# Sums of weights moved into the pooling stage on GpSimd's DMA queue, with later operands, left sums and head norms re-placed

## Chip, cores and metric

The kernel runs on one core of a Trainium2 chip. The metric is the time on the device in microseconds (us) of one launch: three executions were timed, and one more was taken with the hardware profiler. Smaller is better. A core has TensorE (PE, matrix products), VectorE (DVE), ScalarE (ACT), GpSimd (POOL) and SyncE (SP), which here only issues transfers. Each engine executes its own instructions in the order of its own queue.

## What is computed

One layer of a hybrid decoder on 4096 tokens of width 1024, float32:

```python
def rmsnorm(x, w):
    y = xf * lax.rsqrt(jnp.mean(xf * xf, axis=-1, keepdims=True) + EPS)
    return (y * w)

def pool_mixer(u, pool_w, pool_scale):
    cs = jnp.cumsum(uf, axis=1)
    for g, win in enumerate((2, 4, 8, 16)):
        seg = cs[..., 256 * g:256 * (g + 1)]
        prev = jnp.pad(seg, ((0, 0), (win, 0), (0, 0)))[:, :S]
        outs.append((seg - prev) / jnp.minimum(pos, win) - uf[..., 256 * g:256 * (g + 1)])
    return jnp.einsum('bsgc,gcd->bsgd', jnp.stack(outs, axis=2), pool_w) * pool_scale

def mlstm_branch(mx, mz, mo, ...):
    xc = jax.nn.silu(causal_conv(mx, conv_w, conv_b))
    q, k, v = headwise(xc, w_q), headwise(xc, w_k), headwise(mx, w_v)
    h = mlstm_chunkwise(q, k, v, i_pre, f_pre)          # 4 heads, chunks of 128 tokens
    h = jax.nn.sigmoid(mo) * h
    hn = (h - mean(h)) * lax.rsqrt(var(h) + EPS) * mh_norm_w      # per head of 256
    return (hn + m_skip * xc) * jax.nn.silu(mz)

def reference(x, ...):                                  # x: 1 x 4096 x 1024, float32
    u = rmsnorm(x, norm_w)
    proj = u @ w_in                                     # 1024 x 5120
    pool_x, pool_z, m_x, m_z, m_o = the five 1024-wide parts of proj
    y_pool = pool_mixer(pool_x, pool_w, pool_scale) * jax.nn.silu(pool_z)
    y_mlstm = mlstm_branch(m_x, m_z, m_o, ...)
    x = x + jnp.concatenate([y_pool, y_mlstm], axis=-1) @ w_out   # 2048 x 1024
    return rmsnorm(x, final_norm_w)
```

## The kernel before

**Precision.** Every float32 operand of the large products is split into two parts that PE takes at its fast rate: hi is the value cast on ACT, lo is the value less hi, a subtraction on DVE (`split`, L107 to L111; ACT's cast is L110, DVE's subtraction L111). A product is then three matmuls, hi x hi, hi x lo and lo x hi (`mm3`, L113 to L119).

**Pooling stage** (L383 to L575). Eight blocks `b` of 512 tokens. Of each block the tokens are normalised (`norm_u`, begun in the block before) and split (`make_u`). Then eight columns `j` of 128 channels follow: 24 matmuls for pool_x (with pool_w and the scale folded into the weights), 24 for pool_z. ACT copies pool_x into the tile `z` (two buffers), GpSimd copies the last 16 tokens of the column before in front of it and saves its own last 16 (`halo`, L535 and L536), DVE makes the window sums and the product with the gate, and SP stores the result into `yp_d` (L560). PE's two results of a column lie in PSUM banks (`acc`, six buffers). The normalised tokens are stored in `us_d`.

**The four passes** (`drive`, L212) are the large products of the last stage: `o1` (y_pool times the first half of w_out, plus x, into `r_d`), `mo` (u times the m_o columns; gates the mLSTM's result, norms its heads, transposes them on PE with `turned`), `mz` (u times the m_z columns; gives y_mlstm into `ym_d`) and `o2` (y_mlstm times the other half of w_out, plus `r_d`, then the last norm). Each uses a Strassen scheme: seven half-size products in place of eight. Its left operand is four quadrants a11, a12, a21, a22 and four sums of them, s1 to s4 (`A_OF`), its right operand three quadrants of the weights and four sums of quadrants. A pass runs over four rounds `r` of 1024 tokens; a round has 14 steps (seven products `i`, two halves `kh`), each of 24 matmuls. `items` take the results of a product away and add them up (`after`, `done`).

**Where the sums come from.** The left sums of `us_d` and `yp_d` are made in the pooling stage by `sums` (L488 to L509): four loads of 512 KB on SP (L493) into the tiles `st` (four buffers), four operations on GpSimd, four stores (L497). The main loop starts such a job at the columns in `JOBS_AT`; the last one, for `yp_d[-1]` and k = 2, comes behind the loop (L574). The left sums of `ym_d` are made at the end of a quarter of `mz`, four operations on GpSimd in `put_sums` (L198). The sums of `mo`'s and `mz`'s weights are made in the pass `o1`, those of `o2` in the pass `mz`: `stage` (L147) loads four quadrant tiles of 256 KB on SP, makes four sums on GpSimd and stores them in `sums_mo`, `sums_mz` and `sums_o2`; `background` (L1148) places the three parts of such a job at given steps. `o1`'s weights have no stored sums: `load_right` (L121) loads and adds their terms wherever a slot is filled.

**mLSTM stage** (L577 to L958). Its weights, the m_x columns of w_in, are 16 pieces that come through two tiles `ws` (L127) and are split into `wm`. Sixteen steps `project` (256 tokens each) make m_x, the convolution (L656 and around) and more; `front` and `back` process the 32 chunks. When no `project` is left, its place in the order is taken by `next_weights` (L687): `o1`'s first four weight slots, in 17 pieces (`Steps`).

**What sets the order.** The program is written in a given order. A scheduler places each engine's instructions in its queue by readiness and priority, and every engine keeps that order. All loads and stores, other than the left operands `sr` (issued by ACT, L223), are in SP's queue. In `drive`, the left operand of step t + 3 is loaded and that of t + 2 split at step t; `defer` puts something off to the end of a step; `FREE_BANKS` lists the steps of a round at which transposes of `mo` may take PSUM banks, and how many; `prefetch` holds three inputs for them.

## Time and profile before

| | |
|---|---|
| runs | 3162.06, 3155.39, 3155.42 us; median 3155.42 |
| the profiled execution | 3153.02 us; its span 3151.3 us |
| TensorE busy | 2919.7 us (93%), 15912 matmuls |
| VectorE, ScalarE, GpSimd busy | 2089.8, 1373.6, 960.7 us |
| pooling stage, mLSTM, four passes | 0 to 752, 767 to 1757, 1758 to the end |
| HBM | 334.63 MB read, 192.94 MB written |

Busy time counts the engine's own work, not its waits. The times of the rows below count from the start of the span. In the lists of groups, "a<-b" means that a is written from b, "x14" that there are 14 of them; what stands behind `<-` at a wait is the instruction that ended it. L numbers are lines of the kernel before.

### The profile page before, as it was taken

The numbers are of one execution on the slowest core, as the hardware profiler recorded it, in microseconds if no ns is written. First come the engines' busy times: TensorE is split into PE (matmuls) and PEld (weight loads), VectorE is DVE, ScalarE is ACT, GpSimd is POOL, SyncE is SP. The second block draws the span as 40 slices with busy tenths as digits, with TensorE's granted clock in tenths as the row PEclk, the third lists the DMA queues.
The fourth block names the chain that finished last, engine by engine and source line by source line (L and its number), as shares of the span: only waits on it lengthen the run. The fifth ranks groups of instructions, "written<-read, shape, count | busy, mean of one in ns | idle before, by whom it ended". The sixth has DMA issues, their size and how long they took to land. (4 is left out here: it accounts for less than half of the span.)

```text
span 3151.3 us, 45085 instructions
## 1 busy us (share of the span) xinstructions
PE 2919.7 (93%) x15912; PEld 2522.1 (80%) x15912; DVE 2089.8 (66%) x4160; ACT 1373.6 (44%) x2727; POOL 960.7 (30%) x1015
## 2 busy tenths in 40 slices
PE   7999999996989999999997788999998899998998
PEld 6888888885989989989897566887777688876887
DVE  6555555544578878888888553566667766575666
ACT  4222122211577677767666311235556633342332
POOL 1122333333245455445445432001111145321000
PEclk9999999998899999999998899999999999998999
DMA  6344455556121121111113688765666788786654
GB/s 211 124 153 159 155 181 184 184 174 201 46 64 51 48 68 48 61 55 51 61 58 111 227 309 268 238 225 192 209 218 230 260 273 302 260 290 208 213 208 157
DMA packets 256419, 530.55 MB, mean 168 GB/s; under 512 B 28352, under 2 KB 71872, under 8 KB 256192
## 3 DMA queue, kind: packets, MB, share of 16 engines
q1 hardware_dynamic: 223936, 410.21, 37.6%
q10 hardware_dynamic: 32256, 117.45, 11.9%
q8 instruction: 125, 2.05, 0.3%
q14 instruction: 102, 0.84, 0.1%
HBM read 334.63 MB, written 192.94 MB: 167 GB/s over the span
## 5 line engine op out<-in xcount | busy, mean ns | idle before, releaser
L117 PE MATMUL acc<-u,w 128*128 128x512 f32 (+1 forms) x2016 | 691.6, 343 | 2.2 <-ACT u L110 1.8
L119 PE MATMUL acc<-u,w 128*128 128x512 f32 (+1 forms) x2016 | 682.4, 339 | 0.0
L118 PE MATMUL acc<-u,w 128*128 128x512 f32 (+1 forms) x2016 | 680.7, 338 | 0.0
L117 PE MATMUL ps<-w,sr 128*128 128x512 f32 x1344 | 536.7, 399 | 44.4 <-ACT sr L110 29.6
L119 PE MATMUL ps<-w,sr 128*128 128x512 f32 x1344 | 533.6, 397 | 9.2 <-DVE sr L111 9.0
L118 PE MATMUL ps<-w,sr 128*128 128x512 f32 x1344 | 532.5, 396 | 0.0
L111 DVE TENSOR_TENSOR sr<-sr 128x1024 fp32r<-128x1024 f32 x224 | 293.5, 1314 | 304.3 <-ACT sr L110 299.4
L110 ACT CAST sr<-sr 128x1024 fp32r<-128x1024 f32 x224 | 234.2, 1048 | 552.0 <-PE ps L118 293.6
L117 PEld LDWEIGHTS acc<-u,w 128*128 128x128 f32 x2016 | 383.7, 190 | 44.3 <-ACT u L110 2.5
L118 PEld LDWEIGHTS acc<-u,w 128*128 128x128 f32 x2016 | 383.7, 190 | 40.3
L119 PEld LDWEIGHTS acc<-u,w 128*128 128x128 f32 x2016 | 383.5, 190 | 40.2
L117 PEld LDWEIGHTS ps<-w,sr 128*128 128x128 f32 x1344 | 257.9, 192 | 99.6 <-ACT sr L110 32.3
L119 PEld LDWEIGHTS ps<-w,sr 128*128 128x128 f32 x1344 | 257.1, 191 | 69.5 <-DVE sr L111 16.7
L118 PEld LDWEIGHTS ps<-w,sr 128*128 128x128 f32 x1344 | 257.6, 192 | 53.5 <-issue 0.5
L656 DVE SCALAR_TENSOR_TENSOR xc<-mx,col,xc 128x256 f32<-128x256 f32 x384 | 221.2, 632 | 55.4 <-POOL mx L715 46.4
L644 POOL TENSOR_TENSOR cs<-c,cs 128x516 fp32r<-128x516 f32 x124 | 176.4, 1422 | 204.2 <-ACT cs L643 181.7
L1038 POOL TENSOR_TENSOR rs<-rs,nhalf 128x2 f32<-128x2 f32 x64 | 56.0, 876 | 521.0 <-DVE mv L1035 325.9
L117 PE MATMUL ps<-sr,w 128*128 128x512 f32 x448 | 176.5, 394 | 4.3 <-ACT sr L110 3.3
L118 PE MATMUL ps<-sr,w 128*128 128x512 f32 x448 | 176.0, 393 | 1.4 <-DVE sr L111 1.4
L119 PE MATMUL ps<-sr,w 128*128 128x512 f32 x448 | 175.7, 392 | 0.0
L867 PE MATMUL mm<-va,st 128*128 128x258 f32 x384 | 85.6, 318 | 64.2 <-DVE st L111 42.6
L322 DVE TENSOR_TENSOR ch<-ps,ch 128x512 f32<-128x512 f32 x192 | 127.2, 681 | 14.4 <-PE ps L119 13.6
(211 smaller groups left out, 5192.8 us busy)
## 6 DMA issues: line engine op xcount, KB each, us to landing
sr<-us_d ACTq DMA_DIRECT2D x112, 512.0 KB, 5.0
us_d<-st SPq DMA_DIRECT2D x64, 512.0 KB, 2.7
sr<-yp_d ACTq DMA_DIRECT2D x56, 512.0 KB, 5.3
sr<-ym_d ACTq DMA_DIRECT2D x56, 512.0 KB, 4.5
st<-in_x_t_dram SPq DMA_DIRECT2D x32, 512.0 KB, 6.1
yp_d<-sg SPq DMA_DIRECT2D x64, 256.0 KB, 2.5
st<-us_d SPq DMA_DIRECT2D x32, 512.0 KB, 5.8
st<-yp_d SPq DMA_DIRECT2D x32, 512.0 KB, 5.8
```

The source lines that it names most:

```text
L110: nc.scalar.copy(out=hi, in_=raw)
L111: (eng or nc.vector).tensor_tensor(out=lo, in0=raw, in1=hi.bitcast(F32), op=ALU.subtract)
L117: nc.tensor.matmul(ps, lhsT=a[0], rhs=b[0], start=start and k == 0, stop=False, skip_group_check=skip)
L118: nc.tensor.matmul(ps, lhsT=a[0], rhs=b[1], start=False, stop=False, skip_group_check=skip)
L119: nc.tensor.matmul(ps, lhsT=a[1], rhs=b[0], start=False, stop=stop and k == n - 1, skip_group_check=skip)
L322: nc.vector.tensor_tensor(out=v(t), in0=ps, in1=v(t), op=ALU.add)
L644: nc.gpsimd.tensor_tensor(out=t[:, 1], in0=cst[h], in1=t[:, 0].bitcast(F32), op=ALU.subtract)
L656: nc.vector.scalar_tensor_tensor(out=a[:, t], in0=m[:, t, i:i + TB], scalar=conv_w[:, jj * 4 + i:jj * 4 + i + 1], in1=a[:, t], op0=ALU.mul ...
L867: nc.tensor.matmul(nps, lhsT=wt[:, w, h, :], rhs=vh[v], start=i == 0, stop=first and i == 2)
L1038: nc.gpsimd.tensor_tensor(out=rs, in0=rs, in1=nhalf[:, 0:2], op=ALU.pow)
```

## The change

It does five things.

1. *Sums of the right operands.* `stage` is gone, and so is `load_right`. A generator `right_sums` makes all of them, for all four passes, in the pooling stage: 16 row tiles (four passes, four `k`), each with six loads of 256 KB, four subtractions on GpSimd and four stores of 256 KB. The loads and stores are issued by GpSimd, on its own queue, and go through two `ws` tiles. It is called twice in a column from block 1 on (once in each fourth column). In the passes a slot with a sum is filled by two loads of finished values (`Pass.load`, 512 KB each), the plain quadrants are fetched ahead (`Pass.fetch`), and the splits are put off to the end of a step.
2. *Next operands.* `next_operands` takes the place of `next_weights`: beside `o1`'s first four slots it loads and splits the first three left operands of `o1` (`first`), in 11 pieces. Its tiles `xu` (12 buffers) serve the mLSTM stage and the passes. The pools `st` and `ws` are now separate ones in each of the two first stages.
3. *The last left sums* of `yp_d[-1]`, k = 2 and 3, are made in `o1`, round 1 (`last_sums`).
4. *Left sums of `ym_d`:* s1, s2 (GpSimd) and s3 (DVE) are made at the third quadrant, a21; only s4 stays at a12.
5. *Head norm* in `mo`: the power and two small operations are made once for two tiles. `FREE_BANKS` has other steps, and `prefetch` holds four.

The core of the diff:

```diff
-B_OF = (((1, 0, 0),),
-        ((1, 1, 1), (-1, 0, 1), (1, 0, 0)),
-        ((1, 1, 0),),
-        ((1, 1, 1), (-1, 0, 1)),
-        ((1, 0, 1), (-1, 0, 0)),
-        ((1, 1, 0), (-1, 1, 1), (1, 0, 1), (-1, 0, 0)),
-        ((1, 1, 1),))
+B_OF = ((0, 0), None, (1, 0), None, None, None, (1, 1))
 SUM_OF = (None, 1, None, 2, 0, 3, None)
 
-FREE_BANKS = {6: 2, 7: 2, 11: 3, 12: 3, 13: 3, 0: 3, 1: 2}
+FREE_BANKS = {7: 4, 12: 4, 13: 3, 0: 1, 1: 4}
...
-        def stage(self, k, tile):
...
-            nc.gpsimd.tensor_tensor(out=t3, in0=b22, in1=b12, op=ALU.subtract)
-            nc.gpsimd.tensor_tensor(out=b12, in0=b12, in1=b11, op=ALU.subtract)
-            nc.gpsimd.tensor_tensor(out=b22, in0=b22, in1=b12, op=ALU.subtract)
-            nc.gpsimd.tensor_tensor(out=b21, in0=b21, in1=b22, op=ALU.subtract)
-            yield
-            for i, t in enumerate((b12, b22, t3, b21)):
-                nc.sync.dma_start(out=self.sums[i][:, k, :], in_=t)
...
+        def fetch(self, i, tile):
+
+            if SUM_OF[i] is None:
+                (kh, ch), self.raws = B_OF[i], [tile() for _ in range(4)]
+                rows, c0 = self.sources[ch]
+                for k in range(4):
+                    nc.sync.dma_start(out=self.raws[k], in_=rows(k + 4 * kh)[:, c0:c0 + T])
+
+        def load(self, i, pool, tag):
 
             self.slots[i] = hi, lo = [pool.tile([P, 4, T], F32R, name=tag) for _ in range(2)]
...
+            if SUM_OF[i] is not None:
+                for k in (0, 2):
+                    nc.sync.dma_start(out=lo[:, k:k + 2].bitcast(F32), in_=self.sums[SUM_OF[i]][:, k:k + 2, :])
+                return [lambda k=k: split(lo[:, k:k + 2].bitcast(F32), hi[:, k:k + 2], lo[:, k:k + 2])
+                        for k in (0, 2)]
+            raws = self.raws
+            return [lambda k=k: split(raws[k], hi[:, k], lo[:, k]) for k in range(4)]
...
+        for t, pairs in enumerate(first):
+            got[t] = tuple([pair[v] for pair in pairs] for v in range(2))
+        assert len(first) == AHEAD - 1
...
+        def right_sums():
+
+            t, v = (wsp.tile([P, T], F32, name="ws") for _ in range(2))
+            for p in (p_out1, p_o, p_z, p_out2):
+                for k in range(4):
+                    def get(dst, kh, ch):
+                        rows, c0 = p.sources[ch]
+                        nc.gpsimd.dma_start(out=dst, in_=rows(k + 4 * kh)[:, c0:c0 + T])
+
+                    def less(n, a, b):
+                        nc.gpsimd.tensor_tensor(out=a, in0=a, in1=b, op=ALU.subtract)
+                        nc.gpsimd.dma_start(out=p.sums[n][:, k, :], in_=a)
+
+                    get(t, 0, 1)
+                    get(v, 0, 0)
+                    yield
+                    less(0, t, v)
+                    get(v, 1, 1)
+                    yield
+                    less(1, v, t)
+                    get(t, 1, 0)
+                    yield
+                    less(3, t, v)
+                    get(v, 1, 1)
+                    yield
+                    get(t, 0, 1)
+                    yield
+                    less(2, v, t)
...
+                if b and (j + 1) % 4:
+                    next(weights, None)
...
+                if b:
+                    next(weights, None)
...
-        for _ in sums(yp_d[-1], 2):
+        for _ in weights:
...
+        def next_operands():
 
             for i in range(4):
-                yield from p_out1.load(i, w1p, "w1", u_tile)
+                p_out1.fetch(i, x_tile)
+                todo = p_out1.load(i, w1p, "w1")
+                yield
+                for n, f in enumerate(todo):
+                    f()
+                    if n == 1 and len(todo) > 2:
+                        yield
+            for t in range(AHEAD - 1):
+                pairs = []
+                for k in range(2):
+                    hi, lo = x_tile(F32R), x_tile(F32R)
+                    nc.sync.dma_start(out=lo.bitcast(F32), in_=yp_d[0][t // 2][:, 2 * (t % 2) + k, :])
+                    pairs.append((hi, lo))
+                first.append(pairs)
+            yield
+            for pairs in first:
+                for hi, lo in pairs:
+                    split(lo.bitcast(F32), hi, lo)
+                yield
...
+                if self.q % 2 == 0:
                     return
...
+                two = slice(self.q - 1, self.q + 1)
+                rs = wk.tile([P, 2, 2], F32, name="rs")
+                nc.vector.tensor_single_scalar(out=rs, in_=mv[:, two, :, 1], scalar=4 * EPS, op=ALU.add)
+                nc.gpsimd.tensor_tensor(out=rs, in0=rs, in1=nhalf.rearrange("p (a b) -> p a b", a=2), op=ALU.pow)
...
-                if (rh, ch) == (0, 1):
-                    put_sums(ym_d[r], self.c, self.c11, t, self.s1, self.u3, x_tile, nc.gpsimd, store)
+
+                def put(name, t):
+                    store(ym_d[r][A_OF.index(name)][:, self.c, :], t)
+
+                if name == "a21":
+
+                    c11, u3 = self.c11, self.u3
+
+                    def sums():
+                        s1, self.s2 = x_tile(), x_tile()
+                        nc.gpsimd.tensor_tensor(out=s1, in0=t, in1=u3, op=ALU.add)
+                        put("s1", s1)
+                        nc.vector.tensor_tensor(out=t, in0=c11, in1=t, op=ALU.subtract)
+                        put("s3", t)
+                        nc.gpsimd.tensor_tensor(out=self.s2, in0=s1, in1=c11, op=ALU.subtract)
+                        put("s2", self.s2)
+
+                    defer(sums)
+                elif name == "a12":
+                    s4 = x_tile()
+                    nc.gpsimd.tensor_tensor(out=s4, in0=t, in1=self.s2, op=ALU.subtract)
+                    put("s4", s4)
...
+        def last_sums():
+
+            for k in (2, 3):
+                q = {}
+                for name in ("a11", "a12", "a21", "a22"):
+                    q[name] = x_tile()
+                    nc.sync.dma_start(out=q[name], in_=yp_d[-1][A_OF.index(name)][:, k, :])
+                yield
+                put_sums(yp_d[-1], k, q["a11"], q["a12"], q["a21"], q["a22"], x_tile, nc.gpsimd, store)
+                yield
+
...
-            if n in todo and r < NR - 1 and todo[n]:
...
+            if (n, r) == (0, 1) and m in (2, 4, 8, 10):
+                next(more)
...
```

GpSimd's queue in block 1 of the pooling stage (the second of eight), columns 0 to 2, before. `halo` and `z` belong to the columns, `st` to the left sums; what stands behind "waits" are the engines and DMA queues whose semaphores the instruction waits for (DMAHW for queues of SP and ACT, DMASW for GpSimd's own).

```order
L502 TENSOR_TENSOR st_1163<-st_1167,st_1163 128x1024 [waits DMAHW5_49,DMAHW4_49,Pool_49]
L535 COPY z_1196<-halo_136 128x16 [waits DVE_49]
L536 COPY halo_136<-z_1127 128x16 [waits Activation_49]
L504 TENSOR_TENSOR st_1165<-st_1165,st_1167 128x1024 [waits DMAHW7_49]
L506 TENSOR_TENSOR st_1169<-st_1169,st_1165 128x1024 [waits DMAHW5_49,DMAHW0_49,Pool_49]
L535 COPY z_1265<-halo_136 128x16 [waits DVE_49]
L536 COPY halo_136<-z_1196 128x16 [waits Activation_49]
L500 TENSOR_TENSOR st_1305<-st_1303,st_1305 128x1024 [waits DMAHW5_49,DMAHW4_49,DMAHW0_49]
L502 TENSOR_TENSOR st_1303<-st_1307,st_1303 128x1024 [waits DMAHW6_49,Pool_49]
L504 TENSOR_TENSOR st_1305<-st_1305,st_1307 128x1024 [waits DMAHW0_49]
L506 TENSOR_TENSOR st_1309<-st_1309,st_1305 128x1024 [waits DMAHW7_49,DMAHW2_49,Pool_49]
```

and a piece of the changed kernel from the same block, columns 4 to 6, where `ws` are the two tiles of `right_sums` and L495, L498 and L499 its load, subtraction and store:

```order
L498 TENSOR_TENSOR ws_1136<-ws_1136,ws_1135 128x512 [waits DMASW6_49,DMASW5_49]
L499 DMA sums_o1_109<-ws_1136 128x512 [waits Pool_49]
L495 DMA ws_1135<-in_w_in_dram 128x512
L495 DMA ws_1136<-in_w_in_dram 128x512 [waits DMASW7_49]
L498 TENSOR_TENSOR ws_1135<-ws_1135,ws_1136 128x512 [waits DMASW1_49,DMASW0_49]
L499 DMA sums_mo_110<-ws_1135 128x512 [waits Pool_49]
L406 TENSOR_TENSOR rr_1518<-rr_1518,nhalf_70 128x4 [waits DVE_49]
L495 DMA ws_1136<-in_w_in_dram 128x512
L498 TENSOR_TENSOR ws_1136<-ws_1136,ws_1135 128x512 [waits DMASW3_49]
L544 COPY z_1623<-halo_140 128x16
L499 DMA sums_mo_110<-ws_1136 128x512 [waits Pool_49]
L545 COPY halo_140<-z_1553 128x16 [waits Activation_49]
```

The scheduler puts rows of `right_sums` between the two halo copies of columns, and it begins behind column 4 of block 0 and ends ahead of column 3 of block 4, so that all of its rows lie in that stretch.

SP's queue at the end of the pooling stage, before: L127 loads a weight piece of the mLSTM, L560 stores a column, L493 loads for the left sums.

```order
L493 DMA st_5425<-yp_d3_79 128x1024 [waits DMAHW6_49,DMAHW2_49]
L127 DMA ws_5571<-in_w_in_dram 128x512 [waits DMAHW7_49,Activation_49]
L127 DMA ws_5575<-in_w_in_dram 128x512 [waits DMAHW3_49,DMAHW0_49,DVE_49]
L560 DMA yp_d3_79<-sg_5140 128x512 [waits DMAHW1_49,DVE_49]
L127 DMA ws_5579<-in_w_in_dram 128x512 [waits DMAHW7_49,DVE_49]
L127 DMA ws_5583<-in_w_in_dram 128x512 [waits DMAHW0_49,DVE_49]
L127 DMA ws_5587<-in_w_in_dram 128x512 [waits DMAHW4_49,DMAHW2_49,DVE_49]
L127 DMA ws_5591<-in_w_in_dram 128x512 [waits DMAHW5_49,DMAHW3_49,DVE_49]
L127 DMA ws_5595<-in_w_in_dram 128x512 [waits DMAHW6_49,DMAHW4_49,DVE_49]
L560 DMA yp_d3_79<-sg_5211 128x512 [waits DVE_49]
L560 DMA yp_d3_79<-sg_5282 128x512 [waits DVE_49]
```

and after, at the hand-over: L611 loads a weight piece of the mLSTM, L571 stores a column, L632 and L643 load small constants of the mLSTM, L737 the first tokens of `project`.

```order
L611 DMA ws_5781<-in_w_in_dram 128x512 [waits DMAHW0_49,PE_49]
L611 DMA ws_5785<-in_w_in_dram 128x512 [waits DMAHW1_49]
L571 DMA yp_d3_79<-sg_5717 128x512 [waits DMAHW2_49,DVE_49]
L632 DMA bif_5855<-in_b_if_dram 128x8 [waits DMAHW3_49]
L643 DMA st_5862<-in_qkv_cols_dram 128x1024 [waits DMAHW4_49]
L611 DMA ws_5789<-in_w_in_dram 128x512 [waits DMAHW5_49,DMAHW0_49,DVE_49]
L611 DMA ws_5793<-in_w_in_dram 128x512 [waits DMAHW6_49,DMAHW1_49,DVE_49]
L643 DMA st_5863<-in_qkv_cols_dram 128x1024 [waits DMAHW7_49]
L643 DMA st_5864<-in_qkv_cols_dram 128x1024
L611 DMA ws_5797<-in_w_in_dram 128x512 [waits DMAHW5_49,DVE_49]
L611 DMA ws_5801<-in_w_in_dram 128x512 [waits DMAHW6_49,DMAHW2_49,DVE_49]
```

Before, 14 of the 16 weight pieces stand among the last stores of the pooling stage; after, 14 of them stand behind the last left sums of that stage, the last column's store and, further on, among the loads of the first tokens.

ACT's queue at the start of the passes, before: L885 is the last work of the mLSTM, L223 loads a left operand and L110 splits.

```order
L885 ACTIVATE mx_18876<-mm_18878,r_18888 128x256 [waits DVE_49,PE_49]
L223 DMA sr_18926<-yp_d0_76 128x1024 [waits DMAHW3_49,DMAHW4_49,DMAHW2_49,DMAHW5_49,DMAHW1_49,Activation_49]
L223 DMA sr_18929<-yp_d0_76 128x1024
L223 DMA sr_18932<-yp_d0_76 128x1024 [waits DMAHW5_49]
L110 CAST sr_18925<-sr_18926 128x1024 [waits DMAHW7_49]
L110 CAST sr_18928<-sr_18929 128x1024 [waits DMAHW2_49]
L223 DMA sr_18939<-yp_d0_76 128x1024
```

and after, where L922, L192 and L104 are these three:

```order
L922 ACTIVATE mx_19072<-mm_19074,r_19084 128x256 [waits DVE_49,PE_49]
L192 DMA sr_19114<-yp_d0_76 128x1024 [waits DMAHW0_49,DMAHW7_49,Activation_49,Pool_49]
L192 DMA sr_19177<-yp_d0_76 128x1024
L104 CAST w2_19116<-w2_19117 128x1024 [waits DMAHW6_49,DMAHW1_49]
L104 CAST w2_19116<-w2_19117 128x1024 [waits DMAHW2_49]
L104 CAST sr_19113<-sr_19114 128x1024 [waits DMAHW3_49]
L192 DMA sr_19234<-yp_d0_76 128x1024
```

The first three left operands are not loaded and cast there any more; they come from the mLSTM's part of the queue, and the first rows now belong to the fourth operand and to a weight slot with a finished sum.

More of the change, by code (lines that the diff above doesn't have):

```diff
@@ L231, in load, with splits @@
         def load(p, i):
-            for _ in p.load(i, *slot_pool(i), tile):
-                pass
+            def splits(todo):
+                for f in todo:
+                    f()
+            todo = p.load(i, *slot_pool(i))
+            defer(lambda: splits(todo))
         later, fetched = [], []
```

173 lines of the change are left out of this document (74 added, 99 removed).

## The prediction

> **What bounds the kernel now.** The page comes first: the span, and by slices how busy TensorE (PE) and the DMA engines are.
>
> ```profile
> span 3151.3 us, 45085 instructions
> ...
> PE   7999999996989999999997788999998899998998
> ```
>
> The profiled execution took 3153.02 us, 1.7 more than its span and 2.4 less than the median of the runs; all sums below are made against 3153.0. PE is full except at about 760 us (the pooling stage hands over to the mLSTM), in parts of the mLSTM, and again and again after 1750 us. A table by stretches gives the sizes. Its columns are busy us and instructions of PE, its weight loads, VectorE (DVE), ScalarE (ACT) and GpSimd (POOL), then the granted clock, the DMA share and GB/s. A stretch at full pace:
>
> ```profile
> 2000.00:2050.00 50.00, 50.00 (x222) 41.42 (x221) 25.04 (x31) 9.68 (x10) 0.00 (x0) 1.00 0.67 225
> ```
>
> So a matmul takes 50 / 222 = 0.225 us. In the same columns, most of the pooling stage, the hand-over, and the four passes of the last stage (o1, mo, mz, o2):
>
> ```profile
> 111.00:444.00 333.00, 333.00 (x1468) 275.37 (x1467) 189.26 (x245) 71.43 (x125) 103.37 (x94) 1.00 0.49 175
> 752.00:815.00 63.00, 37.02 (x211) 35.09 (x210) 13.75 (x31) 13.96 (x43) 18.52 (x21) 0.65 0.48 155
> 1758.00:2124.00 366.00, 328.20 (x1386) 264.98 (x1385) 190.38 (x235) 83.13 (x93) 73.74 (x48) 0.95 0.80 268
> 2124.00:2503.00 379.00, 348.90 (x1574) 281.33 (x1573) 273.27 (x646) 216.00 (x334) 53.25 (x61) 0.96 0.67 219
> 2503.00:2816.00 313.00, 305.27 (x1334) 250.23 (x1333) 201.65 (x231) 118.61 (x160) 111.86 (x70) 0.99 0.84 284
> 2816.00:3142.00 326.00, 308.85 (x1345) 253.58 (x1343) 217.65 (x331) 102.00 (x187) 40.50 (x43) 0.97 0.58 199
> ```
>
> A pass has 4 x 14 x 24 = 1344 matmuls, 303 us at full pace. The passes stand 63, 76, 10 and 23 us over that: this is what can be won. The pooling stage has PE without a gap at full clock: nothing is to be won there, and what is added there has to stay hidden.
>
> **The passes.** What waited for what in the first 200 us of the first pass (us in total, times, longest):
>
> ```profile
> ACT sr L110 <- DMA sr<-yp_d: 49.5, 11, 10.6
> ...
> PE ps L117 <- ACT sr L110: 29.6, 4, 12.8
> ```
>
> and the small loads and stores issued there (count, size, us to landing):
>
> ```profile
> x<-in_w_in_dram SPq DMA_DIRECT2D x40, 256.0 KB, 5.7
> x<-in_w_out_dram SPq DMA_DIRECT2D x28, 256.0 KB, 5.5
> sums_mo<-x SPq DMA_DIRECT2D x16, 256.0 KB, 5.0
> sums_mz<-x SPq DMA_DIRECT2D x16, 256.0 KB, 3.3
> ```
>
> 12.8 of the 63 us are the first left operand, loaded and split only after the mLSTM; now it is split before, and PE can go on at once. The rest is left operands (sr) that wait among these 100 transfers. Four plain loads stay, four loads of finished sums come, and a pair of left sums in the second quarter. A burst remains at the start, x behind two loads of sums; I leave 13 us for it: **-50** (bounds -63, and -13 if only the first wait goes).
>
> In the second pass, the transposes (count, busy us, mean ns, and the idle time before them by what ended it),
>
> ```profile
> L1069 PE MATMUL ps<-ident,ch 128*128 128x128 f32 x256 | 47.4, 296 | 31.5 <-ACT ch L1043 18.3 <-ACT sr L110 4.2 <-DVE mv L1035 2.9
> ```
>
> and the waits of this pass that a normalised head ended:
>
> ```profile
> PE ps L1069 <- ACT ch L1043: 16.2, 14, 3.0
> ```
>
> Of the 76 us the transposes are 47, which stay; of the other 29, 16.2 are waits for a normalised head. Norm steps over two tiles halve 64 GpSimd powers and twice 64 short DVE operations, but the first tile of a pair now waits for the second. The later slots for the transposes should help more: **-13** (+10 if the pairing delays every group by the longest wait, 3 us, in part of the 16 groups; to -29). Third pass, without 32 transfers for the next sums: **-3** (0 to -10). Last pass, one wait:
>
> ```profile
> PE ps L117 <- DVE ch L989: 14.5, 1, 14.5
> ```
>
> It comes from residual loads that SP holds behind stores, which wait for four GpSimd additions a tile; three of the four now come a quadrant earlier: **-14** (0 to -23).
>
> **The hand-over to the mLSTM.** The last pooling matmul, SP's rows between the two, the first convolution, and the splits of the mLSTM's weight pieces:
>
> ```profile
> 752.29 0.39 PE L119 MATMUL acc<-u,w 128*128 128x512 f32 x1
> ...
> 761.30 0.42 SPq L700 DMA_DIRECT2D u<-us_d  x1
> ...
> 765.87 1.27 SPq L493 DMA_DIRECT2D st<-yp_d  x3
> 772.25 2.74 SPq L497 DMA_DIRECT2D yp_d<-st  x2
> 775.04 0.43 SPq L700 DMA_DIRECT2D u<-us_d  x1
> ...
> 809.73 5.88 DVE L656 SCALAR_TENSOR_TENSOR xc<-mx,col,xc 128x256 f32<-128x256 f32 x12 [46.44 <-POOL mx L715]
> ...
> L110 ACT CAST w<-ws x14: 617/621/626, 702.0 to 757.4; 128x512 fp32r<-128x512 f32 x14
> L111 DVE TENSOR_TENSOR w<-ws,w x14: 676/691/1022, 702.7 to 758.0; 128x512 fp32r<-128x512 f32 x14
> ```
>
> The last pair of left sums (L493, L497) stands between the u loads. It moves to the first pass, and SP is free some 14 us earlier. But the weight pieces that were split inside the last pooling block now come behind it. The price of their loads is in the next rows, with what the pooling stage needs.
>
> **The pooling stage decides the sign.** A 256 KB load inside the pooling stage (two at 109 us: least, median, most), one issued in groups of four, the stores in and after this stage, the issue on SP, the addition on GpSimd, and the additions already in GpSimd's queue:
>
> ```profile
> DMA to landing us min/median/max: 2.7/2.8/3.0
> u<-in_w_out_dram SPq DMA_DIRECT2D x28, 256.0 KB, 3.5
> yp_d<-sg SPq DMA_DIRECT2D x26, 256.0 KB, 2.4
> h_d<-ht SPq DMA_DIRECT2D x62, 256.0 KB, 2.1
> L127 SPq DMA_DIRECT2D ws<-in_w_in_dram x14: 328/330/781, 698.0 to 752.7; - x14
> L129 POOL TENSOR_TENSOR u<-u 128x512 f32<-128x512 f32 x12 | 16.6, 1393 | 11.8 <-DVE rows L790 7.1 <-DMA u<-in_w_out_dram 3.7 <-DVE parts L815 0.9
> L500 POOL TENSOR_TENSOR st<-st 128x1024 f32<-128x1024 f32 x16 | 38.5, 2409 | 116.7 <-DMA st<-us_d 63.9 <-DMA st<-yp_d 52.8
> 110.10 0.20 POOL L536 COPY halo<-z 128x16 f32<-128x16 f32 x1 [14.19 <-ACT z L534]
> ```
>
> For the hand-over: 16 pieces through two buffers are eight rounds of a load (2.7 to 3.5), 0.62, 0.69 and an issue of 0.33, 34 to 41 us from 752, then 8 to 10 us of matmuls: the first convolution at 794 to 803 instead of 809.7 if it waits for all of them, some earlier. SP's other loads there cost part of it: **-6** (-16 to +10). In the mLSTM's end twelve GpSimd additions of 1.4 go and six splits of 0.69 come on DVE, beside PE work: 0.
>
> One row tile's four sums take six loads, four additions and four stores through two buffers. In GpSimd's order each addition waits for a load just issued, and two of the loads for a store just issued. So a tile takes 4 loads + 2 stores + 2 issues + 4 additions, one behind the other. No row shows a DMA that GpSimd issues. From below SP's values bound it (2.7, 2.1, 0.33, 1.4): 21.3 us. From above, the crowded first pass with an issue as long as an addition (5.7, 5.0, 1.4, 1.4): 41.2. I take 3.0, 2.4, 0.7 and 1.4, nearer to the quiet rows because at most two such loads are out at a time: 12 + 4.8 + 1.4 + 5.6 = **23.8 us**, and 381 for 16 tiles. By the Trainium skill (DMA: Bandwidth & Descriptors, Anatomy of one DMA) a DMA of this kind takes about 2.0 us and its bytes at 436 GB/s, an estimate of 2.6 us for 256 KB; with it the tile would be 22.6 us and the forecast 19 us lower; no run so far shows it.
>
> The order puts the 16 tiles between the halo copies of block 0, column 4 (110.10 us), and block 4, column 3: 31 columns of 48 x 0.225 = 10.8 us, 333 at PE's pace. In that stretch GpSimd already has 103 us of work. Most of it falls into the waits; of each of eight jobs of four long additions (2.4) I count 3.4 us as not hidden, 27 in all. 381 + 27 is 75 more than 333. Behind a late GpSimd stand the halo copies, DVE's window sums, and in DVE's queue the next block's splits. z has two buffers, which covers one column, 10.8 us, and the PSUM banks cover about as much; I take 20 us as free (bounds 11 and 54, five columns). So PE stands **+55 us**; each us more on a tile is 16 more.
>
> Sum: -50 - 13 - 3 - 14 - 6 + 55 = -31: **3122 us**.
>
> **The rivals.**
> *GpSimd is overloaded.* With a load of 3.7, a store of 2.8 and an issue of 0.9 a tile takes 27.8: 445 + 27 - 353 = 119 us are lost in the pooling stage, 3153 - 86 + 119 = 3186, slower. It decides from 25.8 us a tile on. For it: loads in groups take 3.5 even in the quiet mLSTM, and this stage has a DMA share of 0.49 before the sums come. Against it: SP's 2.8.
> *All hidden.* At SP's own values, 16 x 21.3 + 27 - 353 = 14 us: 3081.
> *The first pass stays bound by DMA.* Half of the 50 us stays: 3147, no change. For it, the burst at its start; against it, at 2000 us, without those transfers, PE is full at a share of 0.67.
> *DVE holds up GpSimd's issues.* DVE is busy 0.57 of the stretch. If each of 160 issues that meets an operation of 0.9 us waits for half of it, 160 x 0.57 x 0.45 = 41 us come on top: 3163, slower. The Trainium skill (SBUF — State Buffer, Summary: rules for kernel authors) advises ACT or SP for a DMA that lies under DVE work, since GpSimd can't write its descriptors while DVE holds the ports they share. No run so far shows it, and DVE's operations here have two inputs in SBUF, which the same page does not count among those that hold descriptors: little chance.
> That the sums are not moved is no rival: GpSimd's queue holds all 64 before the mLSTM.
>
> **How the numbers follow.** Forecast, a tile of 21.9 to 25.5 us, 3092 to 3149: 0.47. All hidden: 0.15. Overloaded: 0.26. First pass still bound: 0.07. Issues held up: 0.05. About 0.2% is what a measurement can tell from no change; the first pass and the slow edge of the forecast (0.02) lie within it. Faster 0.60, same 0.09, slower 0.31. The range, 3065 to 3195, leaves out passes that gain more than their sum and tiles over 28.4 us, 0.2 together; the far bound of 41 us a tile lies there.
>
> **What would show it.** In the changed profile: GpSimd waits for its own loads in the pooling stage, and their times to landing give the tile's price. PE has gaps there until about block 5, released by halo copies, window sums or splits, and none later. The first pass starts within 3 us of the mLSTM's last matmul and takes about 316 us. The 14.5 us wait at the last pass is gone. The forecast is wrong if PE is full through the pooling stage, if it loses more than 86 us there, or if the four passes together gain less than 40 us.

## The result, and the profile after

The changed kernel takes 3282.12 us (median of 4 runs, 3277.79 to 3284.65) against 3155.6 before: slower, ratio 1.0394 (95% interval 1.0376 to 1.0412). Its profiled execution has a span of 3279.6 us, 128.3 more than before. The page, the span and the rows by slices (40 equal parts of the span):

```profile
span 3279.6 us, 44898 instructions
...
PE   8967576699978999999999979999999999989998
...
POOL 1354453533322445444454421000111012211000
```

TensorE was full in the pooling stage before; now slices 3 to 8, 164 to 656 us, stand at 5 to 7 tenths. That is the stretch in which GpSimd's queue holds the weight sums. A table by stretches, in the columns of the prediction (busy us of PE, its loads, DVE, ACT, POOL, then clock, DMA share, GB/s): the weight sums' stretch, and the four passes:

```profile
108.00:645.00 537.00, 370.84 (x1530) 297.00 (x1528) 188.99 (x248) 71.77 (x128) 272.24 (x320) 0.85 0.57 186
...
1945.00:2269.00 324.00, 317.74 (x1389) 262.33 (x1390) 183.20 (x226) 83.27 (x91) 11.97 (x8) 0.99 0.75 251
2269.00:2642.00 373.00, 348.59 (x1601) 287.16 (x1599) 271.71 (x603) 217.01 (x346) 36.35 (x32) 0.96 0.69 225
2642.00:2972.00 330.00, 317.68 (x1377) 261.15 (x1378) 220.73 (x242) 119.82 (x160) 80.65 (x48) 0.98 0.77 258
2972.00:3270.00 298.00, 290.29 (x1269) 238.09 (x1267) 197.88 (x315) 94.56 (x174) 20.91 (x29) 0.99 0.58 196
```

The 1530 matmuls of the first row need 344 us at 0.225; the stretch took 537. Of the 193 us between, 166 are idle time, and 27 are matmuls that took longer: the granted clock is 0.85 here, where the pooling stage before had 1.00. To compare the passes, take the first result that leaves PSUM in each. It is the same instruction in both kernels: a sum with x or `r_d` on DVE in o1 and o2, the copy of s1 on ACT in mo and mz. Before:

```profile
1781.89 3.67 DVE L989 TENSOR_TENSOR ch<-ps,ch 128x512 f32<-128x512 f32 x6
2129.26 0.58 ACT L310 COPY ch<-ps 128x512 f32<-128x512 f32 x1
2513.69 1.53 ACT L310 COPY ch<-ps 128x512 f32<-128x512 f32 x3
2833.56 3.07 DVE L989 TENSOR_TENSOR ch<-ps,ch 128x512 f32<-128x512 f32 x5
```

After, with the last pooling matmul ahead of them:

```profile
948.43 0.39 PE L113 MATMUL acc<-u,w 128*128 128x512 f32 x1
...
1956.62 1.88 DVE L1023 TENSOR_TENSOR ch<-ps,ch 128x512 f32<-128x512 f32 x3
2268.95 1.57 ACT L286 COPY ch<-ps 128x512 f32<-128x512 f32 x3 [1.99 <-PE ps L113]
2641.52 0.57 ACT L286 COPY ch<-ps 128x512 f32<-128x512 f32 x1
2972.07 1.27 DVE L1023 TENSOR_TENSOR ch<-ps,ch 128x512 f32<-128x512 f32 x2
```

The mLSTM's last output matmul (L867, now L904) begins at 1757.1 before and 1942.6 after. Subtracting the rows gives, in us:

| part | before | after | difference | predicted |
|---|---|---|---|---|
| pooling stage, to its last matmul | 752.7 | 948.8 | +196.1 | +55 |
| hand-over and mLSTM | 1004.4 | 993.8 | -10.6 | -6 |
| to the first result, and o1 | 24.8 + 347.4 | 14.0 + 312.3 | -45.9 | -50 |
| mo | 384.4 | 372.6 | -11.8 | -13 |
| mz | 319.9 | 330.6 | +10.7 | -3 |
| o2, to the end | 317.7 | 307.5 | -10.2 | -14 |

Of the 159 us between the sum of the forecast (-31) and the profile (+128), 141 lie in the pooling stage, 17 in the last two passes. What waited for what there (us in total, times, longest), from 108 us to 660 (PE) and 760 (ACT, DVE and SP's queue):

```profile
PE tp L399 <- ACT sq L104: 119.6, 4, 32.5
PE tp L416 <- ACT sq L104: 31.3, 3, 12.6
PE acc L112 <- DVE u L105: 18.1, 10, 7.7
...
ACT ss L388 <- DMA st<-in_x_t_dram: 179.1, 5, 43.2
...
DVE sum L557 <- POOL z L544: 184.4, 17, 19.1
DVE sq L410 <- POOL rr L406: 69.6, 5, 23.0
...
SPq L476 <- POOL st L479: 156.3, 10, 28.2
```

TensorE stands at `tp`, the normalisation of the next block, for 152 of the 170 us that it waits. Behind it is a chain that leads to GpSimd by two ways. The next block's x_t loads need `st` tiles and a place in SP's queue; both are held by the left sums' stores (L476), which wait for left sums in GpSimd's queue (L479). And the norm's power (L406) is itself an instruction of that queue. VectorE's window sums do wait for the halo copies, as was forecast, and longest of all that VectorE waits for (L557); but no wait of TensorE here was ended by a freed PSUM bank. What GpSimd did from 108 to 645 us (count, busy us, mean ns, idle time before by what ended it), one kind of the left sums' and one of the stores' rows for all, and the times to landing of what it issued:

```profile
L498 POOL TENSOR_TENSOR ws<-ws 128x512 f32<-128x512 f32 x64 | 93.1, 1455 | 187.9 <-DMA ws<-in_w_out_dram 94.7 <-DMA ws<-in_w_in_dram 93.2
L495 POOL DMA_DIRECT2D ws<-in_w_out_dram x48 | 26.3, 547 | 47.0 <-DMA sums_o<-ws 29.4 <-DVE w L105 15.9 <-DMA sums_mz<-ws 1.5
L495 POOL DMA_DIRECT2D ws<-in_w_in_dram x48 | 26.0, 541 | 26.4 <-DMA sums_mo<-ws 11.9 <-DMA sums_mz<-ws 11.7 <-DMA sums_o<-ws 2.2
...
L479 POOL TENSOR_TENSOR st<-st 128x1024 f32<-128x1024 f32 x8 | 19.1, 2383 | 0.1
...
L499 POOL DMA_DIRECT2D sums_o<-ws x32 | 18.2, 567 | 8.9 <-POOL ws L498 8.6 <-POOL z L544 0.3
...
ws<-in_w_out_dram POOLq DMA_DIRECT2D x48, 256.0 KB, 3.9
...
sums_o<-ws POOLq DMA_DIRECT2D x32, 256.0 KB, 3.2
```

That fills the queue: 188 us of waits for loads, 57 for stores, 93 of subtractions, 89 of issues (96 x 0.54 and 64 x 0.57), 17 from a subtraction's end to its store, 76 of left sums (32 x 2.4), some 18 of halo copies and powers: 538 where the stretch has 537 (neighbouring records overlap a little). GpSimd had no time to spare, and TensorE got its pace: 16 tiles of 33.5 us.

### The profile page after: what moved, and what is told of

The parts are those of the page before. It is cut to its first block, busy times and chain, and to the rows that moved or that the text cites. A ratio compares the mean times of both kernels' runs of the same rounds, so it can differ in the third digit from the quotient of the medians.

```text
span 3279.6 us, 44898 instructions
## 1 busy us (share of the span) xinstructions
PE 2930.7 (89%) x15912; PEld 2535.2 (77%) x15912; DVE 2086.6 (64%) x4107; ACT 1371.1 (42%) x2722; POOL 973.6 (30%) x1119
## 4 chain that ended last, share of the span: by engine, by line
PE 55%; DMA 17%; DVE 10%; issue 7%; POOL 7%; ACT 3%; SPq 0%; POOLq 0%; DVEq 0%; ACTq 0%
PE ps L111 7%; PE ps L113 7%; PE ps L112 7%; PE acc L111 7%; PE acc L113 7%; PE acc L112 7%; DMA ws<-in_w_in_dram 5%; DMA ws<-in_w_out_dram 4%; POOL ws L498 3%; DVE xc L676 3%; PE mm L908 2%; PE mm L933 2%; PE mm L904 1%; PE map L787 1%; DMA sums_o<-ws 1%
## 5 line engine op out<-in xcount | busy, mean ns | idle before, releaser
L113 PE MATMUL ps<-w,sr 128*128 128x512 f32 x1320 | 517.8, 393 | 16.4 <-DVE sr L105 16.4
L111 PE MATMUL ps<-w,sr 128*128 128x512 f32 x1320 | 521.9, 395 | 9.1 <-DVE ch L1023 4.7
L112 PE MATMUL ps<-w,sr 128*128 128x512 f32 x1320 | 519.5, 394 | 0.0
L104 ACT CAST sr<-sr 128x1024 fp32r<-128x1024 f32 x221 | 231.6, 1049 | 517.0 <-PE ps L112 379.2
L105 DVE TENSOR_TENSOR sr<-sr 128x1024 fp32r<-128x1024 f32 x221 | 277.8, 1259 | 258.6 <-ACT sr L104 253.8
L112 PE MATMUL acc<-u,w 128*128 128x512 f32 x1024 | 406.3, 397 | 18.2 <-DVE u L105 18.1
L111 PE MATMUL acc<-u,w 128*128 128x512 f32 x1024 | 405.4, 396 | 1.5 <-ACT u L104 1.5
L113 PE MATMUL acc<-u,w 128*128 128x512 f32 x1024 | 404.3, 395 | 0.0
L113 PEld LDWEIGHTS ps<-w,sr 128*128 128x128 f32 x1320 | 250.7, 190 | 70.3 <-DVE sr L105 18.1
L111 PEld LDWEIGHTS ps<-w,sr 128*128 128x128 f32 x1320 | 251.2, 190 | 63.5 <-DVE ch L1023 4.2
L111 PE MATMUL acc<-xu,w 128*128 128x256 f32 x992 | 294.8, 297 | 0.0
L112 PEld LDWEIGHTS ps<-w,sr 128*128 128x128 f32 x1320 | 251.2, 190 | 52.3 <-issue 1.1
L113 PE MATMUL acc<-xu,w 128*128 128x256 f32 x992 | 287.4, 290 | 0.0
L112 PE MATMUL acc<-xu,w 128*128 128x256 f32 x992 | 284.5, 287 | 0.6 <-POOL xu L740 0.5
L112 PEld LDWEIGHTS acc<-u,w 128*128 128x128 f32 x1024 | 196.3, 192 | 65.8 <-DVE u L105 24.5
L111 PEld LDWEIGHTS acc<-u,w 128*128 128x128 f32 x1024 | 196.6, 192 | 43.2 <-ACT u L104 2.2
L113 PEld LDWEIGHTS acc<-u,w 128*128 128x128 f32 x1024 | 195.9, 191 | 40.7
L557 DVE TENSOR_TENSOR sum<-z 128x527 f32<-128x527 f32 x64 | 63.5, 993 | 257.2 <-POOL z L544 184.4
L1080 POOL TENSOR_TENSOR rs<-rs,nhalf 128x4 f32<-128x4 f32 x32 | 36.3, 1136 | 591.2 <-DVE rs L1079 470.9
L112 PEld LDWEIGHTS acc<-xu,w 128*128 128x128 f32 x992 | 193.8, 195 | 1.1 <-POOL xu L740 1.0
```

Source lines behind the costliest of these rows:

```text
L104: nc.scalar.copy(out=hi, in_=raw)
L105: (eng or nc.vector).tensor_tensor(out=lo, in0=raw, in1=hi.bitcast(F32), op=ALU.subtract)
L111: nc.tensor.matmul(ps, lhsT=a[0], rhs=b[0], start=start and k == 0, stop=False, skip_group_check=skip)
L112: nc.tensor.matmul(ps, lhsT=a[0], rhs=b[1], start=False, stop=False, skip_group_check=skip)
L113: nc.tensor.matmul(ps, lhsT=a[1], rhs=b[0], start=False, stop=stop and k == n - 1, skip_group_check=skip)
L557: nc.vector.tensor_tensor(out=nxt[:, a:], in0=cur[:, a:], in1=cur[:, a - step:HALO + T - step], op=ALU.add)
```

## The experiments: the pooling stage

**Pacing.** Each piece of the weight sums is tied behind the halo copy of the column that calls it; the same instructions then spread over 46 columns.

```diff
-                nc.gpsimd.tensor_copy(out=halo[:, j, :], in_=z[:, T:])
+                kept = nc.gpsimd.tensor_copy(out=halo[:, j, :], in_=z[:, T:])
                 if b and (j + 1) % 4:
-                    next(weights, None)
+                    with tc.issue_after(kept.ins):
+                        next(weights, None)
...
```

> Same instructions and transfers as the changed kernel; each piece of the weight sums now stands behind the halo copy of the column at which the program calls it, so the 16 tiles spread over 46 columns (497 us at TensorE's pace) in place of 31. Theory (GpSimd's own time is the bound: 33 us a tile with what else it does, against 21 us that 31 columns leave for one): a tile now has 31 us and about half of its waits fall into the time until the next halo copy, so the pooling stage ends 0 to 50 us after the 752 us of the kernel before instead of 196, and the time is 3085 to 3135 us. Rival (the 42 MB of added traffic slow the stage's own loads): the loss stays, 3250 us or more. Rival (the sums hold the st tiles and so SP's loads of the next block): most of the loss stays too, over 3200.

3182.05 us (1.0076 of before, 1.0048 to 1.0105). The pooling stage ends at 851.7, 99 us late in place of 196. So the number of bytes, of which not one changed, does not set the loss; but the loss that stayed is twice what the theory allowed. Its waits, ACT's for the next block:

```profile
ACT ss L388 <- DMA st<-in_x_t_dram: 171.0, 6, 38.1
```

**The stores alone.** The loads and subtractions are left out; 64 stores of zeros stay on GpSimd's queue.

```diff
+            t = wsp.tile([P, T], F32, name="ws")
+            nc.vector.memset(t, 0.0)
...
+                    for n in range(4):
+                        nc.gpsimd.dma_start(out=p.sums[n][:, k, :], in_=t)
+                        yield
```

> The loads and subtractions of the weight sums are left out, the 64 stores (of zeros) stay on GpSimd's queue, in the place that the scheduler gives them. Theory (the tile's chain of loads, stores and subtractions on GpSimd is the price): the pooling stage ends within 5 us of the 752 us of the kernel before; what is left is the gain of all other parts, hand-over -10 and passes -58: 3085 us (3075 to 3095). Rival (part of the 196 us comes from elsewhere in the stage, such as the separate st and ws pools or SP's other order): it stays over 3105.

3097.22 us, one run, 2 us over the theory's range; the stage ends at 767.9, 15 us late where the theory allowed 5. The scheduler puts all these stores between 100 and 200 us, where the DMA share reaches 0.97, and TensorE's only wait after the first 100 us, 10 us at the norm, lies there. So the loads and subtractions are the price, and all else in the stage, these stores included, comes to 15 us. Whether the loads cost by their bytes or by the waits for them this run can't tell; the last run of this section does.

**Left sums off GpSimd.** As e1, with the four sums of each left-sum job on VectorE.

```diff
-            nc.gpsimd.tensor_tensor(out=a22, in0=a21, in1=a22, op=ALU.add)
+            nc.vector.tensor_tensor(out=a22, in0=a21, in1=a22, op=ALU.add)
...
```

> As e1_paced, with the four sums of each left-sum job of the pooling stage on VectorE in place of GpSimd. In e1_paced the pooling stage still lost some 97 us, and TensorE waited there for the next block's normalisation, whose loads wait for the st tiles of the left-sum jobs. Theory (two jobs of a block stand in GpSimd's queue among pieces that wait for their own loads, hold the st tiles, and so make the next block's loads late): without them in that queue most of the loss goes, 3085 to 3120 us. Rival (GpSimd's pieces themselves are too slow for their columns and hold the halo copies): half of the loss or more stays, 3130 to 3180.

3149.54 us, one run; 66 us late. A third of e1's loss went, not most: the rival's side. The norm still hangs on GpSimd, now by its power, which stands behind pieces that wait for their loads (DVE's wait, and GpSimd's own):

```profile
DVE sq L410 <- POOL rr L406: 75.0, 6, 16.4
...
POOL ws L498 <- DMA ws<-in_w_out_dram: 118.9, 31, 7.2
```

**Three tiles.** As e1, with a third `ws` tile (room for it from `a_u`), four loads a tile, each issued a piece before its use.

```diff
+                get(t, 0, 1)
+                get(v, 0, 0)
+                get(x, 1, 1)
+                yield
+                less(0, v, t, v)
+                yield
+                less(2, t, x, t)
+                less(1, x, x, v)
+                get(v, 1, 0)
+                yield
+                less(3, v, v, x)
+                yield
```

> As e1_paced, with three ws tiles in place of two (a_u has 18 buffers in place of 19 to make room): four loads a row tile in place of six, and a piece's loads are issued a piece before it is used, so GpSimd hardly waits for them. Left sums stay on GpSimd. Theory (GpSimd's waits for its own loads, 157 us in e1_paced, make the jobs and halo copies late): the loss in the pooling stage is 0 to 40 us, time 3085 to 3130. Rival (it is the number of operations and issues in GpSimd's queue, not the waits): the loss stays over 60 us, 3150 or more.

3131.74 us (0.9920, 0.9902 to 0.9939): faster than before, the stage 49 us late. GpSimd's waits for loads fell from 157 to 62 us, and half of e1's loss went with them; the forecast of at most 40 was a little too good. The edit does three things at once (a third tile, 64 loads in place of 96, loads a piece ahead); their shares were not separated. What is left lies again at the turns of blocks.

**Evenly.** As e4, with 9 pieces a block in place of 14, so that they take blocks 1 to 7.

```diff
-                if b and (j + 1) % 4:
+                if b and j == 5:
...
```

> As e4_paced_three (pooling stage 49 us later than before), with 9 pieces a block in place of 14: one in each column and one more in column 5, so that the 64 pieces take all of blocks 1 to 7. Theory (what is left is GpSimd late at the end of each block, so that the next block's normalisation, whose power and st tiles depend on it, is late): with 4 us of piece work a column and 10.8 us a column the loss falls to 0 to 20 us, time 3085 to 3110. Rival (each block pays for the wait of a piece next to the normalisation, wherever the pieces stand): the loss stays at 40 us or more, since all seven blocks are hit, 3125 to 3150.

3096.19 us (0.9813, 0.9793 to 0.9832): the fastest measured, 59 us under the kernel before. The stage ends at 762.3, 10 us late. The whole stage in the columns of the table, GpSimd's subtractions, and TensorE's longest wait at the norm are now

```profile
100.00:762.00 662.00, 657.24 (x2877) 539.78 (x2875) 414.08 (x469) 136.17 (x238) 349.33 (x368) 1.00 0.60 209
...
L499 POOL TENSOR_TENSOR ws<-ws 128x512 f32<-128x512 f32 x62 | 91.7, 1480 | 25.9 <-DMA ws<-in_w_out_dram 15.7 <-DMA ws<-in_w_in_dram 9.7
...
PE tp L399 <- DVE sq L105: 2.5, 2, 1.8
```

This settles the rival of the traffic: the stage carries 209 GB/s at a DMA share of 0.60, more than the changed kernel's stretch (186 at 0.57), GpSimd's loads land no sooner (medians 3.9 and 4.3 us), and TensorE is full. The same sums in the same stage on the same queue cost 196 us or 10, by where they stand and how long each waits; a third tile and a third fewer loads belong to that.

## The experiments: the passes

**The first pass's traffic put back.** The changed kernel, with 32 loads, 32 subtractions and 32 stores of the old `stage` in o1, into tensors that nobody reads.

```diff
+            for i, t in enumerate((b12, b22, t3, b21)):
+                nc.sync.dma_start(out=spare[p.name][i][:, k, :], in_=t)
...
+            if n == 0 and r < NR - 1 and todo:
+                if m in (2, 7, 11):
+                    next(todo[0])
```

> The changed kernel with the first pass's work on weight sums of before put back beside it: 32 loads, 32 subtractions on GpSimd and 32 stores of 256 KB in the first three quarters of o1, into tensors that nobody reads. Theory (these transfers made the left operands late): the first pass is 20 to 40 us longer than the 312 us between its first and the second pass's first eviction in the changed kernel, total 3302 to 3322. Rival (its gain came from operands split ahead and from the weights' finished sums): within 8 us of the changed kernel.

3322.68 us, one run: 41 more. The pass takes 354.9 in place of 312.3, 2.6 us over the theory's range, at the DMA share and the rate that it had before (0.80, 268):

```profile
1945.00:2313.00 368.00, 330.80 (x1384) 265.90 (x1383) 184.83 (x229) 83.85 (x92) 61.18 (x40) 0.95 0.80 266
```

ACT's waits for left operands, first of the changed kernel, then of this one:

```profile
ACT sr L104 <- DMA sr<-yp_d: 35.8, 10, 5.9
```

```profile
ACT sr L104 <- DMA sr<-yp_d: 84.0, 20, 7.3
```

The gain of o1 came from moving this work out. That the transfers did it, and not the 32 subtractions, rests on these waits, which the operands' loads ended.

**First operands late.** The changed kernel without the three left operands split inside the mLSTM.

```diff
-        for t, pairs in enumerate(first):
-            got[t] = tuple([pair[v] for pair in pairs] for v in range(2))
+        for t in range(AHEAD - 1):
+            issue(t)
+        for t in range(AHEAD - 2):
+            make(t)
```

> The changed kernel without the first three left operands split inside the mLSTM; they are loaded and split at the start of the passes as before. From the mLSTM's last output matmul to the first eviction it took 24.8 us before and 14.0 in the changed kernel. Theory (TensorE waits there for the first operand's load and split): 24 to 27 us again, the rest of the first pass as in the changed kernel (312 us), total 3291 to 3296. Rival (the later waits move with it): the first pass is shorter by as much, total within 3 us of 3282.

3294.51 us, one run, 12 more. From the mLSTM's last output matmul to the first result it is 23.7 us again, the theory's place and 0.3 us under its range; the rest of o1 gave 5 back (307.1), and mo took 4 more (376.7). Hand-over and mLSTM, which no theory spoke of, took 6.8 more, so that the total lies in the theory's range is in part chance; the 9.7 us of the start are what the run shows.

**Head norm and its steps.** Two undos: the norm for each tile again, and the old steps and three prefetched inputs.

```diff
-                rs = wk.tile([P, 2, 2], F32, name="rs")
...
+                rs = wk.tile([P, 2], F32, name="rs")
...
```

> The changed kernel with the head norm's power and small operations made for each tile again; the steps for the transposes stay the changed kernel's. The second pass took 384 us before and 372.6 in the changed kernel. Theory (part of the 12 us comes from the pairing): second pass 375 to 380 us. Rival (the transposes' other steps do it all): 371 to 374 us. Total of the changed kernel 3282 plus the same difference.

```diff
-FREE_BANKS = {7: 4, 12: 4, 13: 3, 0: 1, 1: 4}
+FREE_BANKS = {6: 2, 7: 2, 11: 3, 12: 3, 13: 3, 0: 3, 1: 2}
...
-            while later and len(fetched) < 4:
+            while later and len(fetched) < 3:
```

> The changed kernel with the steps for the transposes (FREE_BANKS) and the three prefetched inputs of the kernel before; the paired norm stays. The second pass took 384 us before, 372.6 in the changed kernel and 379 with the norm made for each tile. Theory (pairing and steps bring about half each): second pass 376 to 381 us, total 3282 plus the same difference. Rival (the steps bring nothing, and the rest of the 12 us came with fewer transfers): 371 to 375 us.

3291.87 and 3300.69 us, one run each. The second pass, whose length lies between 370.7 and 376.7 us in the eleven kernels here that leave it as the change has it:

| mo, us | old steps | new steps |
|---|---|---|
| norm for each tile | 384.4 (before) | 379.3 |
| norm for two tiles | 390.7 | 372.6 (after) |

The first lies in its theory's range, the second outside of both. With pairing, the new steps and the fourth input are worth 18 us, far more than the pass differs by itself. At the new steps pairing gains 7, of which the spread leaves 3 certain. That it costs 6 at the old ones is not shown as well: the kernel before differs from the other three in more than the norm (its slots are loaded and split in another order). The first tile of a pair waits for the second, and later transposes hide this. The transposes' waits for a normalised head, with the old steps and in the changed kernel, and the transposes of the changed kernel (to set beside the row that the prediction shows; four of 256 records are missing):

```profile
PE ps L1112 <- ACT ch L1087: 27.2, 19, 4.1
```

```profile
PE ps L1112 <- ACT ch L1087: 16.1, 8, 4.7
...
L1112 PE MATMUL ps<-ident,ch 128*128 128x128 f32 x252 | 39.2, 293 | 18.0 <-ACT ch L1087 16.1 <-DVE xu L1114 1.0 <-DVE rs L1079 0.7
```

Against the kernel before, the idle time ahead of the transposes fell from 31.5 to 18.0 us, but the part that a normalised head ended only from 18.3 to 16.1: what went are the waits for splits and for short VectorE operations.

**The turn from the third to the last pass.** mz and o2 together: 637.6 us before, 638.1 after. Three tries: the left sums of `ym_d` as before; in e5, the last pass's lo halves on GpSimd; in e5, s3 on GpSimd.

```diff
-                    defer(sums)
...
+                if (rh, ch) == (0, 1):
+                    put_sums(ym_d[r], self.c, self.c11, t, self.s1, self.u3, x_tile, nc.gpsimd, store)
```

> The changed kernel with the left sums of ym_d made as before, four on GpSimd at the end of a quarter. Theory (s3 on VectorE waits for s1 on GpSimd, which reads the tile that s3 overwrites, and the splits queue behind it; that cost the third pass 10 us in its last round): third pass 10 us shorter than in the changed kernel (about 320), the wait at the start of the fourth returns (fourth pass 5 to 10 us longer), total within 5 us of the changed kernel's 3282. Rival (the third pass lost its 10 us to the later transposes or to o2's operands): third pass as in the changed kernel, total 5 to 15 us longer.

```diff
+            eng = nc.gpsimd if self.name == "o2" else None
...
-            return [lambda k=k: split(raws[k], hi[:, k], lo[:, k]) for k in range(4)]
+            return [lambda k=k: split(raws[k], hi[:, k], lo[:, k], eng) for k in range(4)]
```

> As e5_three_even, with the lo halves of the last pass's weights subtracted on GpSimd, which is idle there, in place of VectorE. Third and fourth pass together took 638 us before, in the changed kernel and in c1_left_sums_late alike. Theory (VectorE, 9 to 10 of 10 us busy at the turn from the third to the fourth pass, bounds it; the left sums of ym_d do not): the two passes take 625 to 632 us, time 6 to 13 us below e5_three_even. Rival (the turn waits for transfers, of r_d and of the weights): within 3 us of e5_three_even.

```diff
-                        nc.vector.tensor_tensor(out=t, in0=c11, in1=t, op=ALU.subtract)
+                        nc.gpsimd.tensor_tensor(out=t, in0=c11, in1=t, op=ALU.subtract)
```

> As e5_three_even, with the left sum s3 of ym_d on GpSimd in place of VectorE, at the same place (a21). In e5_three_even TensorE waits once 8.7 us for a split that stands in VectorE's queue behind four s3, each of which waits for GpSimd's s1 of the same tile. Theory (that wait is what the third pass lost): third and fourth pass together 626 to 632 us in place of 637, time 5 to 10 us below e5_three_even (3096). Rival (the turn is bound by transfers and by VectorE's splits and evictions, as c1_left_sums_late and e6_even_o2_pool suggest): the wait moves, the two passes take 634 to 640 us, time within 4 us of e5_three_even.

3281.58 us (one run), 3105.34 (0.9845, 0.9826 to 0.9865) and 3103.48 (0.9836, 0.9814 to 0.9859); mz and o2 together 638.2, 642.8 and 643.4, where e5 has 636.7. All three theories fell, and so did their rivals: c1 is not 5 to 15 us longer, and the other two differ from e5 by 9 and 7 us where 3 and 4 were allowed. In the changed kernel TensorE's wait at the turn looked like a plain case: a split in DVE's queue behind s3 (L1162), which waits for GpSimd (L1160). TensorE's wait, and DVE's rows ahead of it:

```profile
PE ps L113 <- DVE sr L105: 9.7, 1, 9.7
```

```profile
2949.02 0.69 DVE L1162 TENSOR_TENSOR ch<-ch 128x512 f32<-128x512 f32 x1 [1.15 <-POOL xu L1160]
2949.63 1.75 DVE L1146 TENSOR_TENSOR ch<-ch,xu 128x512 f32<-128x512 f32 x1
2951.30 1.21 DVE L105 TENSOR_TENSOR sr<-sr 128x1024 fp32r<-128x1024 f32 x1
```

With s3 on GpSimd the like wait of e5 (8.7) is gone, and others stand there, 14.5 us in all:

```profile
PE ps L113 <- DVE sr L105: 5.3, 4, 2.7
PE ps L111 <- ACT sr L104: 4.6, 1, 4.6
PE ps L111 <- DVE ch L1023: 4.6, 4, 2.0
```

Something else sets the time there. Around the turn of e5 four stretches of 10 us have a DMA share of 1.02 or 1.03, so it may be the transfers (residuals from `r_d`, sums of o2's weights, the stores of `ym_d`). That wasn't tried: it stays open.

## Why the prediction was wrong

**The mechanism was named, its price was not.** The forecast of 3122 rested on the pooling stage at +55; it came to +196. The rival "GpSimd is overloaded" describes what happened, but with other terms: its 27.8 us a tile come mostly from longer transfers, 20.4 us, and these took 17.9. The step that failed is the price of a tile, 23.8 us, with 27 us in all for what isn't hidden. The stretch gives it back, term by term:

- *Issues:* two of 0.7 us were counted, since only these stood in the chain of data. But each of the ten issues occupies GpSimd for 0.54 or 0.57 us: 5.5 us in place of 1.4, the largest error. The queue's chain is not the data's chain.
- *Transfers* were priced well. Where no left sum stood between a load's issue and its subtraction (50 of 64 times) GpSimd waited 3.6 us; with 3.5 us a tile for stores that is 17.9 against 12 + 4.8 in the forecast. About 1 us a tile more goes from each subtraction's end to its store's issue, which the forecast left out; the subtractions took 5.8 in place of 5.6.
- *The tile by itself* so comes to 30.3 us, and 104 us more for 16.
- *Left sums:* 27 of 103 us of GpSimd's other work were counted as not hidden. In the stretch it was 76 us of left sums and 18 of small work. 19 of the 32 left sums stood between a load's issue and its subtraction, and these 14 subtractions waited 0.6 us in place of 3.6: an estimate of 41 us hidden (14 x 2.96), 53 not, 26 more than forecast. An in-order queue hides other work in a wait only where that work stands between the issue and the wait.
- *Cover:* 20 us were taken as free (z's buffers and PSUM banks); 537 - 196 - 333 leaves 8. The prediction looked at the halo copies, the window sums and the splits. What TensorE stood at was the normalisation of the next block, which none of these buffers covers, and which needs GpSimd twice.

Tiles and left sums make 130 us (the stretch itself: 537 - 408 = 129), and 12 us of missing cover the rest of the 141 between +55 and +196. The range ended at 28.4 us a tile, with a chance beyond it that was too small: the far bound of 41.2 us was in the text, and the value taken stood near the other end.

**"DVE holds up GpSimd's issues"** can be dropped for the issues. Those of the 48 loads of w_out have a least and a median of 536 ns and a longest of 755; but among GpSimd's subtractions there are long ones:

```profile
L495 POOL DMA_DIRECT2D ws<-in_w_out_dram x48: 536/536/755, 108.3 to 635.5; - x48
...
L498 POOL TENSOR_TENSOR ws<-ws x64: 1255/1283/5697, 112.3 to 642.0; 128x512 f32<-128x512 f32 x64
...
418.56 5.70 POOL L498 TENSOR_TENSOR ws<-ws 128x512 f32<-128x512 f32 x1 [4.46 <-DMA ws<-in_w_in_dram]
...
421.22 1.88 DVE L105 TENSOR_TENSOR u<-st,u 128x512 fp32r<-128x512 f32 x3
```

The longest began inside a row of VectorE's operations that had no gap from 413.9 to 423.1, and ended 1.2 us after it; two of the next three ended in the same way. Over their median the 64 subtractions took 11 us in all. What VectorE holds there was not tested.

The page SBUF — State Buffer of the Trainium skill (Summary: rules for kernel authors) warns that GpSimd's descriptors starve while VectorE is in one of its faster modes; in this stretch, with VectorE busy for 0.35 of it, the trace shows no such hold in the issues, and no run here tells those modes from others.

**The first pass:** -45.9 for -50, by the mechanism that was given; c2 shows it (+42.6 with the work back), c5 shows the start (9.7). "The first pass stays bound by DMA" was wrong.

**The second pass:** -11.8 for -13. The sum was right, its mechanism only in part: of the waits for a normalised head, 2 us went, and 11 of the gain in idle time are other waits that ended with the new steps and the new order. So the right number is partly luck. Pairing and steps are not independent: with pairing the waits for a head are 27.2 us at the old steps and 16.1 at the new ones.

**The third and the last pass:** -17 predicted, +0.5 measured. The 14.5 us wait went, as forecast, and the turn takes as long as before. The step that failed is "it comes from residual loads that SP holds behind stores, which wait for four GpSimd additions a tile": with these additions late again (c1, one run) the wait does not come back (the longest of its kind there is 3.5 us), and the two passes take the same 638. So the wait went for another reason, and without it others stand at the turn; which of them set its time stays open.

**The hand-over:** -10.6 for -6, within its bounds; it was not tested by itself.

## What to carry to other kernels

An in-order queue that issues a load and then waits for it is priced by all that the queue does: every issue, every wait and every other job behind it; its idle time is free only for work that stands between the issue and the wait. Before work goes into an "idle" engine, ask which of its other instructions the next block needs (here a power and the left sums), and look at where the scheduler really puts it: the same sums cost 196 us bunched into half of the stage and 10 us when spread over it, through three tiles, with their loads one piece ahead. The worth of one edit can hang on another (pairing and later steps), so undo them singly and together. And a wait that went is not yet time won: see whether it returns when the edit is undone, and whether the stretch got shorter.

## What the runs showed of the hardware

In the changed kernel a 256 KB DMA occupies GpSimd for 0.54 us (a load) or 0.57 us (a store); in the kernel before, the issue of such a load took SP 0.33 us. Its loads landed after 3.7 us (median; least 2.7, longest 8.0) at a DMA share of 0.57. The Trainium skill (DMA: Bandwidth & Descriptors, Anatomy of one DMA) gives 2.0 us and the bytes at 436 GB/s, an estimate of 2.6 us; the trace agrees with it as the least, not as the usual time in a busy stage.
